# A decoder trunk on one core: fewer whole feed-forward tiles around the pairs, and the mixer's squares beside them

## The chip, the cores and the metric

The kernel runs on one core of a Trainium2 chip. The core has a matrix engine (TensorE, PE in the profile), three engines for elementwise work (VectorE or DVE, ScalarE or ACT, GpSimd or POOL), queues that issue transfers (the issues on SP and POOL matter here) and 16 DMA engines. The metric is the device time of one execution in microseconds (us), less is better. Each engine runs its instructions in the order in which the program was built, and an instruction that waits holds up all that stand behind it on its engine.

## The reference

A trunk of two layers on one sequence of 1024 tokens with 1024 channels, all in float32. Layer 0 mixes tokens with a causal convolution module, layer 1 with trailing means over windows of 2, 4, 8 and 16 tokens. Each mixer is followed by a SwiGLU feed-forward of width 2816. Each part is wrapped in an RMS norm, a shift and scale from a conditioning vector c, and a gated residual.

```python
for i in range(DEPTH):                       # 2 layers
    mod = silu(c) @ ada_w[i] + ada_b[i]
    sh_m, sc_m, g_m, sh_f, sc_f, g_f = split(mod, 6)
    h = rms_norm(x, norm_mix_g[i]) * (1 + sc_m) + sh_m
    y = conformer_conv(h, ...) if i == 0 else multiscale_pool(h, ...)
    x = x + (1 + g_m) * y
    h = rms_norm(x, norm_ffn_g[i]) * (1 + sc_f) + sh_f
    y = (silu(h @ w_gate) * (h @ w_up)) @ w_down        # 1024 -> 2816 -> 1024
    x = x + (1 + g_f) * y
return rms_norm(x, final_g)
```

## The kernel before, in words

**Halves.** The tokens are two chunks, A and B, of 512, held as x[chunk][k], eight tiles of 128 channels by 512 tokens. There are four feed-forward halves, and PE runs them in the order A0, B0, A1, B1 (chunk and layer). Between B0 and A1 lies A's pooling mixer, between A1 and B1 that of B. Work of the other chunk (its statistics, its mixer, a late piece of its feed-forward) is run inside a half.

**Products.** A float32 factor is split into a rounded part "hi" and a remainder "lo", and a product is three matmuls, hi·hi, hi·lo and lo·hi. The activations of a half are hhi and hlo (8 tiles each), those behind the SwiGLU ghi and glo. Each matmul is recorded at line 123, each operation of DVE, ACT and POOL at line 101, so the tiles' names (gate, up, dn, y, hhi, w, raw) tell the rows apart.

**Plain tiles.** The width is 22 f-tiles of 128. A plain f-tile (`ffn_p1`) is 24 matmuls of 512 columns for gate and 24 for up, then t = silu(gate) on ACT, t·up on DVE, ghi on ACT and glo on DVE or POOL. A down pass (`ffn_p2`) takes two f-tiles: eight output groups dn of 6 matmuls, each followed by an update of x on DVE. The weights of a plain tile come through `load_weight`: SP loads a tile raw (L398), ACT writes hi (a CAST) and minus raw (an ACTIVATE) into two of the nine buffers w, and POOL issues an accumulating load onto the second (L403), which leaves the lo part. ACT's write waits until PE has let go of the buffer.

**Pairs.** Between its first and its last plain tiles a half computes gate and up for two f-tiles at once by a 2×2 scheme with seven quarter products in place of eight ("f-pair" below; the gate or the up of one is a "mate", `ffn_pair`). A quarter product is 12 matmuls of 256 columns, so a mate is 84. It needs sums of quarters of the activations, called T (`combined`: hf = hi + lo, tf the sums, thi and tlo their parts, in rows k = 0 to 3; t1 to t4 are its columns), and sums of quarters of the weights (`Pair.prepare`: acc and ny on DVE from the raw tiles, then shi and slo; also two accumulating loads at L946). The first quarter product uses the activations as they are, the second already needs t1. Each mate carries four output groups of an earlier f-pair's down pass (24 matmuls of 512 columns). ACT copies the quarter products out of the accumulators (COPY t<-gate), DVE adds them.

**Order.** PE's order is that of the program text: a list of units (`unit`), each a tile, a down pass or a pair. `put` starts a task whose steps are spread beside the units that follow, when a planner's clocks for the engines let them (`pace`), and `need` asks that a task be done. The order on the other engines comes from a scheduler that ranks instructions by where they stand in the program. `PLAIN` is the count of whole tiles ahead of the pairs, `UNTIL` the tile at which a half's pairs end, `OUT_AT` the unit behind the pairs at which the mixer's output product y (`pool_out`) stands. `pool_stats` squares the other chunk's x on ACT, adds the squares on DVE into acc and starts the norm of its mixer: PE sums the columns (var), DVE takes the root (col), PE spreads it (rstd). `norm` does the same for a feed-forward and then makes hhi on ACT and hlo on DVE (`modulated`). Until B0's end DVE also computes layer 1's modulation (adaw, "ada dots" of 1024 columns, loaded at L133).

**Buffers.** `window` has three buffers shared by the mixer's sums, hf, sg and, in the change, pq; tag "acc" has two, shared by squares and by two of a mate's four weight sums.

Of the kernel before, what the change touches and what calls it, by code (L numbers as in the profile page):

```python
# [19 lines left out]
KT = D // P  # L20
# [26 lines left out]
STRETCH = 1.35  # L47
LATER = 300
PREPARED = 120
PLAIN = 4  # L50
UNTIL = (16, 16, 20)
OUT_AT = 6
DELAY = {"stats": 2.75, "spread": 1.5}
DELAY_BEHIND = {"stats": 8, "spread": 4}

# [51 lines left out]
def trunk(ctx, tc, xT, c, vec, ada, adan, w1, w2, wgu, wdn, wpl, out):  # L107
# [148 lines left out]
    def temp(n, name="t", bufs=0):  # L256
        t = tmp.tile([P, TMPW], F32, tag=name if bufs else "t", name=nm(name), bufs=bufs or 4)
        return t[:, :n]

    def window(n, name):  # L260

        t = tmp.tile([P, PHALO + TMPW], F32, tag="win", name=nm(name), bufs=3)
        return t[:, :n]
# [191 lines left out]
    class Squares:  # L455
# [5 lines left out]
        def add(self, k):  # L461
            ch = self.ch
            if self.acc is None:
                self.acc = bank("acc") if self.psum else temp(ch.n, "acc", 2)
                S_.activation(self.acc, x[ch.i][k], AF.Square)
            else:
                sq = temp(ch.n)
                S_.activation(sq, x[ch.i][k], AF.Square)
                was = self.acc
                if self.psum and k == KT - 1:  # L470
                    self.acc = temp(ch.n, "acc", 2)
                V_.tensor_tensor(self.acc, was, sq, op=ADD)

    def sum_sq(srcs, n):
        acc = None
        for s in srcs:
            if acc is None:
                acc = temp(n, "acc", 2)
                S_.activation(acc, s, AF.Square)
            else:  # L480
                sq = temp(n)
                S_.activation(sq, s, AF.Square)
                V_.tensor_tensor(acc, acc, sq, op=ADD)
            yield
        return acc
# [41 lines left out]
    def unit(emit, *weights):  # L527
        units.append((weights, emit))
# [333 lines left out]
    def combined(ch):  # L862

        other = chunks[1 - ch.i]
        h = st["h", ch.i]
        got = st["T", ch.i] = []
        for k in range(KT // 2):
            whole = []
            for hi, lo in (h[k], h[k + KT // 2]):
                t = window(ch.n, "hf")  # L870
                V_.tensor_tensor(t, f32(hi), f32(lo), op=ADD)
                whole.append(t)
            a, b = whole
            q12, q34 = temp(ch.n, "tf"), temp(ch.n, "tf")
            V_.tensor_tensor(q12[:, LEFT], a[:, LEFT], a[:, RIGHT], op=SUB)
            V_.scalar_tensor_tensor(q12[:, RIGHT], q12[:, LEFT], -1.0, b[:, RIGHT], op0=MUL, op1=SUB)
            V_.tensor_tensor(q34[:, LEFT], b[:, RIGHT], a[:, RIGHT], op=SUB)
            V_.scalar_tensor_tensor(q34[:, RIGHT], q12[:, RIGHT], -1.0, b[:, LEFT], op0=MUL, op1=SUB)
            yield
            row = []  # L880
            for q in (q12, q34):
                hi, lo = slot(other, "thi"), slot(other, "tlo")
                S_.copy(hi, q)
                V_.tensor_tensor(lo, q, f32(hi), op=SUB)
                row += [(hi[:, LEFT], lo[:, LEFT]), (hi[:, RIGHT], lo[:, RIGHT])]
            got.append(row)
            yield
# [184 lines left out]
    def ffn_mixed(ch, l, until, at_end=False):  # L1072

        before = []
        for f in range(0, PLAIN, 2):
            before += [ffn_p1(ch, l, f, True, False), ffn_p1(ch, l, f + 1, True, False)]
            if f:
                before.insert(-1, ffn_p2(ch, l, [f - 2, f - 1], True))
        mates = [Pair(ch, l, f, which) for f in range(PLAIN, until, 2) for which in range(2)]
        mine, theirs = [None] * len(mates), []  # L1080
        for i, f in enumerate(range(PLAIN - 2, until - 2, 2)):
            first, second = Downs(ch, l, (f, f + 1), (0, 1)), Downs(ch, l, (f, f + 1), (2, 3))
            for at, d in ((2 * i + 1, first), (2 * i + 2, second)):
                if at < len(mates):
                    mine[at] = d
                else:
                    theirs.append(d)
        last, = theirs
        paired = [(lambda take: mates[0].prepare(), ())]
        for i, me in enumerate(mates):  # L1090
            if i + 1 == len(mates):
                paired.append((lambda take: reserve.__setitem__(0, 2), ()))
            paired.append(ffn_pair(ch, l, me, mates[i + 1] if i + 1 < len(mates) else None, mine[i], (mine + [last])[i + 1]))
        paired.append((lambda take: last.load(last.dps[1]), ()))
        rest = ffn(ch, l, True, at_end, until, ffn_p2(ch, l, [until - 2, until - 1], True))
        rest[1:1] = [alone(last)]
        return before, paired, rest
# [123 lines left out]
    T = {}  # L1221

    def put(name, gen, urgent=False):
        def emit(take):
            T[name] = Task(gen(), urgent)
        unit(emit)

    def need(*names):
        unit(lambda take: finish(*(T[n] for n in names)))
# [58 lines left out]
    for i, (e, ws) in enumerate(fa):  # L1288
        if i == len(fa) - OUT_B:
            need("ln_b")  # L1290
            sq_b = Squares(B)
            conv_out(B, sq_b)
            unit(lambda take: T.__setitem__("norm_bf", Task(norm(B, 0, True, ("h", 1), squares=sq_b), True)))
        unit(e, *ws)
    need("norm_bf")
    unit(lambda take: stretch.__setitem__(0, 1.0))


    def pool_stats(ch):
        acc = yield from sum_sq(x[ch.i], ch.n)  # L1300
        steps = st["spread", ch.i] = mean_rsqrt(acc, ch.n, True, "col2")
        for said in steps:
            if said == "spread":
                break
            yield said
# [27 lines left out]
        need(("nf", ch.i))  # L1333
        unit(lambda take: st.__setitem__(("h", ch.i), st["hn", ch.i]))

    def paired(ch, us):
        need(("T", ch.i))
        add(us)

    before, pairs, rest = ffn_mixed(B, 0, UNTIL[0])  # L1340
    put(("T", 1), lambda: combined(B))
    add(before[:2])
    put(("stats", 0), lambda: pool_stats(A))
    add(before[2:])
    need(("stats", 0))
    paired(B, pairs)
    pooled(rest[:-1], A, OUT_AT)
    before, pairs, rest_a = ffn_mixed(A, 1, UNTIL[1])
    add(before[:1] + rest[-1:])
    put(("T", 0), lambda: combined(A))  # L1350
    add(before[1:2])
    put(("stats", 1), lambda: pool_stats(B))
    add(before[2:])
    need(("stats", 1))
    paired(A, pairs)
    pooled(rest_a[:-1], B, OUT_AT)
    before, pairs, rest = ffn_mixed(B, 1, UNTIL[2], True)
    add(before[:1] + rest_a[-1:])
    put(("T", 1), lambda: combined(B))
    add(before[1:])  # L1360
    put("final_a", lambda: final(A))
    paired(B, pairs)
    add(rest)
    run_units(W_BUFS, early)


# [42 lines left out]
```

## Time and profile before

| what | value |
|---|---|
| median of 3 runs | 1856.09 us (1854.83 to 1858.48) |
| the profiled execution | 1855.7 us, span 1853.9 us |
| mean granted TensorE clock | 0.983 |
| busy: PE, DVE, ACT, POOL | 95%, 72%, 56%, 32% of the span |
| norm of B0 (from its rstd at 714.0) and the late down passes of A0 | to 742.8 us |
| B0: whole tiles; pairs; whole tiles with A's mixer | 742.8 to 798.9; to 982.6; to 1102.1 us |
| A1: the same, with B's mixer | 1102.1 to 1169.3; to 1350.2; to 1468.7 us |
| B1: whole tiles; pairs; the rest | 1468.7 to 1535.5; to 1782.2; to 1853.9 us |

Times within the profile count from the first instruction. A row of the trace gives start, duration, engine, line, operation, output<-inputs, shape and, in brackets, how long the engine stood idle before it and what released it. PE's matmuls overlap in the records (each takes longer than the distance to the next), so its pace is read from starts.

### The profile page before, as it was taken

The page shows a single profiled execution, that of the slowest core. Times are in us where ns is not written, and L with a number is a line of the kernel's source. Part 1 is how long each engine was busy: PE and PEld are TensorE (multiplying, and loading weights), DVE is VectorE, ACT ScalarE, POOL GpSimd, SP SyncE. Part 2 cuts the span into 40 slices and gives each one's busy share as a digit, 9 for nine tenths or more (in the row PEclk, how much of TensorE's full clock was granted, in tenths as well). Part 3 has the DMA queues.
Part 4 walks back from the last instruction along what each step waited for, and adds up shares of the span by engine and source line. Part 5 has one row for each costly group of instructions (what it writes and reads, how often), then busy time and mean ns, then how long its engine had stood idle before and what let it go on. Part 6 is the DMA issues. An engine that isn't in the chain of part 4 may idle for free.

```text
span 1853.9 us, 25885 instructions
## 1 busy us (share of the span) xinstructions
PE 1770.2 (95%) x9544; PEld 1506.3 (81%) x9544; DVE 1325.7 (72%) x2147; ACT 1044.6 (56%) x1613; POOL 596.7 (32%) x636
## 2 busy tenths in 40 slices
PE   6999939999999999999999999999999999999996
PEld 4666628788888887889998788999988889999985
DVE  8788872897876326889978547778684468887736
ACT  3656645866665554655555555555555546555543
POOL 3478731777762311211115221111151221111111
PEclk9999959999999999999999999999999999999998
DMA  7968828889798798977765977655568876655562
GB/s 258 296 199 244 209 47 181 215 203 239 197 240 207 202 240 185 241 212 206 201 190 126 223 170 185 172 136 137 136 140 212 181 169 168 177 136 137 128 135 68
DMA packets 114801, 340.62 MB, mean 184 GB/s; under 512 B 11377, under 2 KB 21745, under 8 KB 114674
## 3 DMA queue, kind: packets, MB, share of 16 engines
q1 hardware_dynamic: 75792, 221.51, 35.9%
q0 software_dynamic: 37728, 116.41, 35.1%
q8 instruction: 75, 1.23, 0.3%
q10 hardware_dynamic: 1154, 1.05, 0.2%
q14 instruction: 52, 0.43, 0.1%
HBM read 334.73 MB, written 4.19 MB: 183 GB/s over the span
## 4 chain that ended last, share of the span: by engine, by line
PE 81%; DVE 7%; DMA 6%; issue 2%; ACT 2%; POOL 1%; SPq 0%; DVEq 0%; POOLq 0%; ACTq 0%
PE dn L123 22%; PE up L123 22%; PE gate L123 21%; PE y L123 6%; PE a L123 3%; PE g L123 2%; PE first L123 2%; DMA adaw<-in_adan_dram 2%; DMA raw<-in_wgu_dram 2%; DMA w<-in_wdn_dram 1%; DVE x L101 1%; ACT w L101 1%; DVE t L101 1%; DMA w<-in_wgu_dram 1%; PE ada L123 1%
## 5 line engine op out<-in xcount | busy, mean ns | idle before, releaser
L123 PE MATMUL dn<-ghi,w 128*128 128x512 f32 (+1 forms) x1440 | 471.4, 390 | 2.7 <-DMA w<-in_wdn_dram 1.3
L101 ACT ACTIVATE w<-raw 128x1024 fp32r<-128x1024 f32 (+1 forms) x262 | 243.0, 928 | 319.0 <-PE dn L123 95.9
L101 ACT CAST w<-raw 128x512 fp32r<-128x512 f32 (+1 forms) x392 | 322.3, 824 | 144.4 <-PE up L123 53.5
L101 DVE SCALAR_TENSOR_TENSOR x<-dn,gains,x 128x512 f32<-128x512 f32 (+1 forms) x360 | 263.1, 735 | 81.9 <-PE dn L123 79.1
L123 PEld LDWEIGHTS dn<-ghi,w 128*128 128x128 f32 x1440 | 270.7, 190 | 56.0 <-DMA w<-in_wdn_dram 2.1
L123 PE MATMUL gate<-hhi,w 128*128 128x512 f32 (+1 forms) x1088 | 310.8, 359 | 3.1 <-DMA w<-in_wgu_dram 2.6
L123 PE MATMUL up<-hhi,w 128*128 128x512 f32 (+1 forms) x1088 | 310.1, 358 | 0.0
L123 PE MATMUL dn<-glo,w 128*128 128x512 f32 (+1 forms) x720 | 279.9, 389 | 0.9 <-POOL glo L101 0.9
L101 POOL TENSOR_TENSOR pa<-pa,pr 128x512 f32<-128x512 f32 x175 | 239.0, 1445 | 24.4 <-ACT pr L101 21.9
L946 POOL DMA_DIRECT2D w<-in_wgu_dram x80 | 69.8, 872 | 493.4 <-ACT w L101 157.4
L123 PEld LDWEIGHTS gate<-hhi,w 128*128 128x128 f32 x1088 | 196.5, 189 | 35.4 <-DMA w<-in_wgu_dram 3.5
L123 PEld LDWEIGHTS up<-hhi,w 128*128 128x128 f32 x1088 | 196.7, 189 | 30.5
L123 PE MATMUL gate<-hlo,w 128*128 128x512 f32 (+1 forms) x544 | 195.1, 359 | 1.1 <-DVE hlo L101 1.1
L123 PE MATMUL up<-hlo,w 128*128 128x512 f32 (+1 forms) x544 | 194.6, 358 | 0.0
L403 POOL DMA_DIRECT2D w<-in_wgu_dram x96 | 86.5, 901 | 321.5 <-ACT w L101 297.8
L101 DVE SCALAR_TENSOR_TENSOR ca<-u,vecs,ca 128x512 f32<-128x512 f32 x273 | 186.6, 747 | 0.1
L101 DVE TENSOR_TENSOR t<-t,up 128x512 f32<-128x512 f32 (+1 forms) x88 | 55.0, 625 | 166.4 <-PE up L123 153.6
L123 PEld LDWEIGHTS dn<-glo,w 128*128 128x128 f32 x720 | 137.2, 191 | 23.8 <-POOL glo L101 1.2
L101 ACT ACTIVATE pr<-u,vecs 128x512 f32<-128x512 f32 x175 | 117.9, 716 | 13.4 <-POOL pa L101 5.9
L123 PEld LDWEIGHTS gate<-hlo,w 128*128 128x128 f32 x544 | 102.7, 189 | 17.6 <-DVE hlo L101 1.9
L123 PEld LDWEIGHTS up<-hlo,w 128*128 128x128 f32 x544 | 102.7, 189 | 15.6
L101 DVE TENSOR_TENSOR w<-raw,w 128x512 fp32r<-128x512 f32 (+1 forms) x122 | 84.5, 700 | 30.3 <-ACT w L101 27.2
(178 smaller groups left out, 3368.1 us busy)
## 6 DMA issues: line engine op xcount, KB each, us to landing
raw<-in_wgu_dram SPq DMA_DIRECT2D x176, 512.0 KB, 5.2
w<-in_wgu_dram POOLq DMA_DIRECT2D x96, 512.0 KB, 8.1
raw<-in_wdn_dram SPq DMA_DIRECT2D x88, 512.0 KB, 5.5
adaw<-in_ada_dram SPq DMA_DIRECT2D x64, 512.0 KB, 6.0
w<-in_wdn_dram POOLq DMA_DIRECT2D x48, 512.0 KB, 8.5
raw<-in_w_dram SPq DMA_DIRECT2D x44, 512.0 KB, 6.6
w<-in_wgu_dram POOLq DMA_DIRECT2D x80, 256.0 KB, 5.7
w<-in_w_dram POOLq DMA_DIRECT2D x34, 512.0 KB, 8.5
```

The source lines that it names most:

```text
L101: self.last = self.order(getattr(self.eng, name)(out, *args, **kw))
L123: last_mm[0] = nc.tensor.matmul(out, lhsT, rhs, start=start, stop=stop, **kw).ins.name
L403: order(nc.gpsimd.dma_start(as_src(lo), src, accum_op=ADD))
L946: order(nc.gpsimd.dma_start(lo, src, accum_op=ADD))
```

## The change

`PLAIN` goes from 4 to 2, `UNTIL` from (16, 16, 20) to (18, 18, 20), `OUT_AT` from 6 to 4. So each half has two whole tiles ahead of its pairs; B0 and A1 have four behind them, and B1 two as before. B0 and A1 have eight f-pairs in pair form in place of six each, and B1 nine in place of eight.

The three halves now go through one function, `segment`. In it the unit that is left over from the half before (`late`, the down pass of tiles 20 and 21) stands behind the first whole tile. For A1 and B1 that is its old place; for B0 it stood ahead of the norm's `need`, directly behind the other down passes of A0. T's task starts ahead of the first tile (it started behind the late pass in A1 and B1), T is asked for ahead of the pairs, and the squares of `pool_stats` start only then, beside the pairs, where they were beside the whole tiles. Their sum is a `window` called pq in place of a buffer acc.

What this does to DVE in B0, between the norm and the first pair. Before, behind the last updates of x by A0's tiles 18 and 19 (hf and tf make T; adaw is an ada dot):

```order
L101 SCALAR_TENSOR_TENSOR adaw_1060_5694,mod_136<-adaw_1060_5694,cact_75 128x1024
L101 SCALAR_TENSOR_TENSOR x_0_2_79<-dn_1134_6049,gains_137,x_0_2_79 128x512
L101 SCALAR_TENSOR_TENSOR x_0_3_80<-dn_1135_6057,gains_137,x_0_3_80 128x512
L101 TENSOR_TENSOR hf_1147_6114<-hhi_1079_5810,hlo_1080_5811 128x512
L101 TENSOR_TENSOR hf_1148_6116<-hhi_1087_5818,hlo_1088_5819 128x512
L101 SCALAR_TENSOR_TENSOR x_0_4_81<-dn_1136_6065,gains_137,x_0_4_81 128x512
L101 TENSOR_TENSOR tf_1149_6118<-hf_1147_6114 128x256
L101 TENSOR_TENSOR tf_1150_6119<-hf_1148_6116,hf_1147_6114 128x256
L101 SCALAR_TENSOR_TENSOR x_0_5_82<-dn_1137_6073,gains_137,x_0_5_82 128x512
L101 SCALAR_TENSOR_TENSOR tf_1149_6118<-tf_1149_6118,hf_1148_6116 128x256
```

In the changed kernel, from the same ada dot on:

```order
L101 SCALAR_TENSOR_TENSOR adaw_1060_5694,mod_136<-adaw_1060_5694,cact_75 128x1024
L101 TENSOR_TENSOR hf_1135_6062<-hhi_1079_5810,hlo_1080_5811 128x512
L101 TENSOR_TENSOR hf_1136_6064<-hhi_1087_5818,hlo_1088_5819 128x512
L101 TENSOR_TENSOR tf_1137_6066<-hf_1135_6062 128x256
L101 TENSOR_TENSOR tf_1138_6067<-hf_1136_6064,hf_1135_6062 128x256
L101 SCALAR_TENSOR_TENSOR tf_1137_6066<-tf_1137_6066,hf_1136_6064 128x256
L101 TENSOR_TENSOR acc_1203_6342<-raw_1172_6218 128x512
L101 TENSOR_TENSOR acc_1209_6354<-raw_1171_6216,raw_1172_6218 128x512
L101 SCALAR_TENSOR_TENSOR tf_1138_6067<-tf_1137_6066,hf_1136_6064 128x256
L101 SCALAR_TENSOR_TENSOR adaw_1097_5841,mod_136<-adaw_1097_5841,cact_75 128x1024
```

The updates by the late down pass have moved behind the start of T, and the weight sums of the first mate (acc from raw) and a second ada dot stand among T's first row.

ACT in A1, from the norm on. Before (ny is the spread rstd, hhi the eight activations, w the weights' parts):

```order
L101 COPY ny_1808_9613<-rstd_1807_9608 128x512
L101 ACTIVATE hhi_1768_9430<-t_1809_9615,mod_136 128x512
L101 ACTIVATE hhi_1770_9432<-t_1810_9619,mod_136 128x512
L101 ACTIVATE hhi_1772_9434<-t_1811_9623,mod_136 128x512
L101 ACTIVATE hhi_1774_9436<-t_1812_9627,mod_136 128x512
L101 ACTIVATE t_1815_9633<-gate_1800_9533 128x512
L101 ACTIVATE w_1833_9728<-raw_1831_9725 128x1024
L101 CAST w_1835_9734<-raw_1834_9732 128x1024
L101 ACTIVATE hhi_1776_9438<-t_1824_9666,mod_136 128x512
L101 CAST ghi_1813_9631<-t_1815_9633 128x512
L101 ACTIVATE hhi_1778_9440<-t_1825_9682,mod_136 128x512
L101 ACTIVATE hhi_1780_9442<-t_1826_9686,mod_136 128x512
```

In the changed kernel, from the first hhi on:

```order
L101 ACTIVATE hhi_1831_9781<-t_1872_9966,mod_136 128x512
L101 ACTIVATE hhi_1833_9783<-t_1873_9970,mod_136 128x512
L101 ACTIVATE hhi_1835_9785<-t_1874_9974,mod_136 128x512
L101 ACTIVATE hhi_1837_9787<-t_1875_9978,mod_136 128x512
L101 ACTIVATE t_1878_9984<-gate_1863_9884 128x512
L101 ACTIVATE w_1898_10082<-raw_1896_10079 128x1024
L101 CAST w_1901_10092<-raw_1900_10090 128x1024
L101 ACTIVATE w_1902_10093<-raw_1900_10090 128x1024
L101 CAST w_1929_10202<-raw_1928_10200 128x1024
L101 CAST ghi_1876_9982<-t_1878_9984 128x512
L101 ACTIVATE hhi_1839_9789<-t_1889_10035,mod_136 128x512
L101 ACTIVATE hhi_1841_9791<-t_1892_10055,mod_136 128x512
```

The fifth to eighth hhi stood behind two weight writes (the eighth a little later), and stand now behind four of them and a ghi. The order in B1 moves in the same way.

```diff
--- before.py
+++ after.py
@@ -47,9 +47,9 @@
 STRETCH = 1.35
 LATER = 300
 PREPARED = 120
-PLAIN = 4
-UNTIL = (16, 16, 20)
-OUT_AT = 6
+PLAIN = 2
+UNTIL = (18, 18, 20)
+OUT_AT = 4
 DELAY = {"stats": 2.75, "spread": 1.5}
 DELAY_BEHIND = {"stats": 8, "spread": 4}
 
@@ -1291,13 +1291,20 @@
             sq_b = Squares(B)
             conv_out(B, sq_b)
             unit(lambda take: T.__setitem__("norm_bf", Task(norm(B, 0, True, ("h", 1), squares=sq_b), True)))
-        unit(e, *ws)
+        if i < len(fa) - 1:
+            unit(e, *ws)
     need("norm_bf")
     unit(lambda take: stretch.__setitem__(0, 1.0))
 
 
     def pool_stats(ch):
-        acc = yield from sum_sq(x[ch.i], ch.n)
+        acc = window(ch.n, "pq")
+        S_.activation(acc, x[ch.i][0], AF.Square)
+        for k in range(1, KT):
+            yield
+            sq = temp(ch.n)
+            S_.activation(sq, x[ch.i][k], AF.Square)
+            V_.tensor_tensor(acc, acc, sq, op=ADD)
         steps = st["spread", ch.i] = mean_rsqrt(acc, ch.n, True, "col2")
         for said in steps:
             if said == "spread":
@@ -1333,34 +1340,27 @@
         need(("nf", ch.i))
         unit(lambda take: st.__setitem__(("h", ch.i), st["hn", ch.i]))
 
-    def paired(ch, us):
+    def segment(ch, l, until, late, at_end=False):
+
+        other = chunks[1 - ch.i]
+        before, pairs, rest = ffn_mixed(ch, l, until, at_end)
+        put(("T", ch.i), lambda: combined(ch))
+        add(before[:1] + late + before[1:])
         need(("T", ch.i))
-        add(us)
-
-    before, pairs, rest = ffn_mixed(B, 0, UNTIL[0])
-    put(("T", 1), lambda: combined(B))
-    add(before[:2])
-    put(("stats", 0), lambda: pool_stats(A))
-    add(before[2:])
-    need(("stats", 0))
-    paired(B, pairs)
-    pooled(rest[:-1], A, OUT_AT)
-    before, pairs, rest_a = ffn_mixed(A, 1, UNTIL[1])
-    add(before[:1] + rest[-1:])
-    put(("T", 0), lambda: combined(A))
-    add(before[1:2])
-    put(("stats", 1), lambda: pool_stats(B))
-    add(before[2:])
-    need(("stats", 1))
-    paired(A, pairs)
-    pooled(rest_a[:-1], B, OUT_AT)
-    before, pairs, rest = ffn_mixed(B, 1, UNTIL[2], True)
-    add(before[:1] + rest_a[-1:])
-    put(("T", 1), lambda: combined(B))
-    add(before[1:])
-    put("final_a", lambda: final(A))
-    paired(B, pairs)
-    add(rest)
+        if at_end:
+            put("final_a", lambda: final(other))
+        else:
+            put(("stats", other.i), lambda: pool_stats(other))
+        add(pairs)
+        if not at_end:
+            need(("stats", other.i))
+            pooled(rest[:-1], other, OUT_AT)
+            return rest[-1:]
+        add(rest)
+
+    late = segment(B, 0, UNTIL[0], fa[-1:])
+    late = segment(A, 1, UNTIL[1], late)
+    segment(B, 1, UNTIL[2], late, True)
     run_units(W_BUFS, early)
```

## The prediction

> **What bounds the kernel now.** I read the page's busy shares first, then the table of waits on TensorE (PE) for the part that the change touches, then the windows by stage, then single rows.
>
> ```profile
> PE 1770.2 (95%) x9544; PEld 1506.3 (81%) x9544; DVE 1325.7 (72%) x2147; ACT 1044.6 (56%) x1613; POOL 596.7 (32%) x636
> PE 81%; DVE 7%; DMA 6%; issue 2%; ACT 2%; POOL 1%; SPq 0%; DVEq 0%; POOLq 0%; ACTq 0%
> ```
>
> PE is busy 95% of the span, and the chain that ends last is PE for 81%. Next, what PE waits for from 717 us on (us in total, times, longest), and the windows (us; busy us and count on PE, PEld, DVE, ACT, POOL; clock; DMA share; GB/s):
>
> ```profile
> PE var L123 <- DVE acc L101: 6.4, 2, 4.6
> PE rstd L123 <- DVE col L101: 3.8, 2, 2.5
> PE gate L123 <- DMA w<-in_wgu_dram: 2.6, 2, 1.9
> PE gate L123 <- ACT t L101: 2.1, 1, 2.1
> ...
> 742.80:798.90 56.10, 55.77 (x249) 45.87 (x248) 46.13 (x86) 33.76 (x52) 16.58 (x18) 1.00 0.91 233
> 889.30:920.40 31.10, 31.10 (x217) 29.03 (x216) 28.50 (x48) 16.97 (x35) 4.83 (x7) 1.00 0.72 204
> 1200.00:1231.10 31.10, 31.10 (x219) 29.05 (x218) 24.73 (x41) 17.05 (x33) 3.48 (x4) 1.00 0.54 140
> ```
>
> These four, the largest, add up to 14.9 us of 1137, and the longest of them lie at the very end, which the change leaves alone. The granted clock is full (1.00). So two things can move the time: PE's own work, and new waits. The third row is one f-pair (two f-tiles of 128 columns) in pair form in half B0: PE is full, and DVE is busy 28.50 of 31.10 us, so DVE has little room there. In A1 (last row) it has 24.73.
>
> **Fewer matmul columns.** UNTIL less PLAIN gives (18−2)/2 + 8 + 9 = 25 f-pairs in pair form against 6+6+8 = 20. Spacings on PE:
>
> ```profile
> 736.17 0.39 PE L123 MATMUL dn<-glo,w 128*128 128x512 f32 x1
> 742.35 0.39 PE L123 MATMUL dn<-glo,w 128*128 128x512 f32 x1
> 804.23 0.28 PE L123 MATMUL gate<-tlo,shi 128*128 128x256 f32 x1
> 804.35 0.28 PE L123 MATMUL gate<-thi,slo 128*128 128x256 f32 x1
> 1102.14 0.39 PE L123 MATMUL gate<-hhi,w 128*128 128x512 f32 x1
> 1113.02 0.40 PE L123 MATMUL dn<-ghi,w 128*128 128x512 f32 x1
> ```
>
> Starts count, since the modelled ends overlap. A plain tile of gate and up is 48 matmuls, 1102.14 to 1113.02, 10.88 us; a down pass over two tiles is 48 matmuls at (742.35 − 736.17)/27 = 0.229, 10.99 us. A plain f-pair is thus 2 × 10.88 + 10.99 = 32.75. In pair form it is 168 matmuls of 256 columns (two mates of 7 × 12) and the same 48 downs, and the window at 889.30 shows 217 matmuls in 31.10, so 216 take about 31.06. The gain is 1.69 an f-pair, times five **−8.45**.
>
> The Trainium skill, "TensorE: Matmul & The Clock Gate", section "Back-to-back issue gap", gives a sustained 81 ns a matmul at 128 columns and 131 ns at 512 for a stream with weight loads; an estimate between them of some 97 ns at 256 would make pair form dearer (168 × 97 against 96 × 131 ns, 3.7 us an f-pair), and five f-pairs +18.6 in place of −8.45. The trace differs, 227 ns at 512 and 120 ns at 256 columns, and its spacings decide.
>
> **B0, from the norm to the first pair.** The late down pass of tiles 20 and 21 of A0 (2 weight loads on SP, 4 casts on ACT, 2 accumulating loads on POOL, 48 matmuls, 8 updates on DVE) moves behind the first tile of B0, and two plain tiles and a down pass go. PE stands thus before:
>
> ```profile
> 729.86 0.40 PE L123 MATMUL dn<-ghi,w 128*128 128x512 f32 x1
> 731.24 0.51 PE L123 MATMUL dn<-ghi,w 128*128 128x512 f32 x1 [0.99 <-ACT ghi L101]
> 732.62 0.49 PE L123 MATMUL dn<-glo,w 128*128 128x512 f32 x1 [0.87 <-POOL glo L101]
> 804.01 0.38 PE L123 MATMUL gate<-thi,shi 128*128 128x256 f32 x1 [2.06 <-ACT t L101]
> ```
>
> The moved pass loses its two waits (1.38 − 0.23 = 1.15 each, −2.3), since its operands are then ten us old. PE starts B0's gate at 729.3, the late pass at 740.2, the second tile at 751.2, the first pair at 762.0; 12 matmuls of its first quarter product and 9 of the second later, at 764.5, it wants the last row of t1 from DVE. DVE's order before that row has 64 instructions after the update that ends at 731.65: 6 ada dots, 8 updates, 16 of 256 columns and 34 of 512. Their spacings:
>
> ```profile
> 730.25 1.40 DVE L101 SCALAR_TENSOR_TENSOR x<-dn,gains,x 128x512 f32<-128x512 f32 x2
> 735.43 1.22 DVE L101 SCALAR_TENSOR_TENSOR adaw<-adaw,cact 128x1024 f32<-128x1024 f32 x1
> 736.57 0.08 DVE L101 DVE_READ_ACCUMULATOR adaw<-adaw,cact 128x1 f32 x1
> 740.04 0.42 DVE L101 TENSOR_TENSOR tf<-hf 128x256 f32<-128x256 f32 x1
> 740.38 0.42 DVE L101 TENSOR_TENSOR tf<-hf,hf 128x256 f32<-128x256 f32 x1
> 771.83 0.68 DVE L101 TENSOR_TENSOR acc<-acc,t 128x512 f32<-128x512 f32 x1
> 772.43 0.68 DVE L101 TENSOR_TENSOR ny<-acc,raw 128x512 f32<-128x512 f32 x1
> 732.18 0.33 SPq L398 DMA_DIRECT2D raw<-in_wgu_dram  x1
> raw<-in_wgu_dram SPq DMA_DIRECT2D x176, 512.0 KB, 5.2
> 786.51 0.69 DVE L101 TENSOR_TENSOR acc<-raw 128x512 f32<-128x512 f32 x1 [4.36 <-DMA raw<-in_wgu_dram]
> ```
>
> The dot is 736.57 − 735.43 = 1.14, the update 1.40 − 0.74 = 0.66, the narrow one 0.34, the wide one 0.60: 6 × 1.14 + 8 × 0.66 + 16 × 0.34 + 34 × 0.60 = 38.0, so 769.6. Among them stand the sums of the first mate's weights, reached at 735.0, and their raw tile is issued only at about 732.2 and lands 5.2 later: 2.4 more, and behind that waiting instruction stands all of T. That makes 772.1, a wait of 7.6 for PE. Without the DMA part it is 5.2; with the 4.36 that such a sum waited at 786.51, 9.6. I take 7.6, since the median landing is of just this kind of load. The old start of the pairs had 2.1 at 804.01 (for a copy on ACT), and this vanishes under the longer wait. Net 7.6 − 2.3 − 2.1 = **+3.2** (0.8 to 5.2).
>
> **A1, from the norm to the first pair.** Between rstd and the gate of A1 there stood two plain tiles (the first begun) and a down pass:
>
> ```profile
> 1079.35 0.83 PE L123 MATMUL rstd<-ident,col 128*128 128x128 f32 x6
> 1082.62 2.71 ACT L101 ACTIVATE hhi<-t,mod 128x512 fp32r<-128x512 f32 x4 [0.82 <-DVE t L101]
> 1101.43 1.06 ACT L101 ACTIVATE w<-raw 128x1024 fp32r<-128x1024 f32 x1 [6.00 <-PE dn L123]
> 1104.29 1.03 ACT L101 CAST w<-raw 128x1024 fp32r<-128x1024 f32 x1
> 1114.76 0.73 PE L123 MATMUL dn<-ghi,w 128*128 128x512 f32 x2 [0.42 <-DMA w<-in_wdn_dram]
> 1481.79 0.73 PE L123 MATMUL dn<-ghi,w 128*128 128x512 f32 x2 [0.85 <-DMA w<-in_wdn_dram]
> ```
>
> Before, all eight hhi stood ahead of the block of weight casts that waits for the last down group (1101.43, four casts, done at 1105.3, 3.2 after the gate's start at 1102.14). With one tile less behind rstd, ACT's order has that block, and a ghi, between hhi 4 and hhi 5. At some 0.6 each for the ghi and the hhi (four took 2.71 at 1082.62), hhi 5 is done 4.4 after the gate's start and its hlo, after a hand-over to DVE, at 5.6, while PE wants that hlo after 13 matmuls, at 2.95: 2.65. Of the next three, whose hlo on DVE stand among sums of raw weights, the sixth adds 0.65, the seventh 1.5 (behind such a sum) and the eighth 0.55: **5.4** in all; with no sum in the way 3.9, with a raw tile 3 us late 8.4. The late pass behind that tile loses its 0.4 (1114.76). The squares, now beside the pairs, put two adds ahead of what ACT's first copies of the quarter products wait for: +1.5 (0 to 3). Net 5.4 − 0.4 + 1.5 = **+6.5** (3.5 to 11.0).
>
> The Trainium skill speaks against this step: the same page, section "Architectural detail: the array is 16× 32×32, not 1× 128×128", has ACT and DVE as strict first-in first-out queues, so that no hhi passes a waiting cast. The trace agrees: ACT stood idle for the 6.00 us ahead of 1101.43, whatever stood behind that cast. Were it otherwise, the sum would be that of rival (a).
>
> **B1, from the norm to the first pair.** The same order on ACT; without the two sums among the hlo it is 3.9 and 0.4 for the later eighth, 4.3, and the 0.9 at 1481.79 goes: **+3.4** (1 to 5). T is far enough ahead here and in A1, as DVE has no ada dots left.
>
> **The mixers and the pairs.** OUT_AT of 4 puts y some 39 us behind the pairs' end instead of 63:
>
> ```profile
> 982.56 1.05 PE L123 MATMUL rstd<-ident,col 128*128 128x128 f32 x8
> 1024.26 0.73 PE L123 MATMUL gate<-hhi,w 128*128 128x512 f32 x2 [1.88 <-DMA w<-in_wgu_dram]
> 1025.92 0.69 DVE L101 TENSOR_TENSOR mxlo<-win,mxhi 128x512 fp32r<-128x512 f32 x1 [0.17 <-ACT mxhi L101]
> 1045.81 0.39 PE L123 MATMUL y<-mxhi,w 128*128 128x512 f32 x1
> ```
>
> The last mxlo is done 44 us behind 982.56, and y's last group wants it some 48 behind: nothing on the path, with 4 us to spare; the 2.0 at 1024.26 passes to another weight. The squares (7 adds at 0.60 on DVE, 8 on ACT, and a dozen tiny ones) and five more f-pairs' 28 DVE instructions each lie beside pairs with 2.6 us (B0) or 6.4 (A1) of room an f-pair; I put +0.5 on B0 (0 to 3), where the room is least.
>
> **Sum.** −8.45 + 3.2 + 6.5 + 3.4 + 0.5 = +5.15. The profiled execution took 1855.7 (span 1853.9 and 1.8 around it), 0.4 below the median of 1856.1; on the profiled execution that makes 1860.9, from the median 1861.2.
>
> **Rivals.** (a) Faster: ACT's blocks of casts find their buffers free early, so that hhi 5 to 8 are never held. For it: ACT was idle for 6.00 us ahead of 1101.43, so it has the time. Against it: the block stands on the last down group directly ahead of the gate. It gives 5.15 − 5.4 − 4.3 = −4.55, 1851.5; it decides once the block ends 2.65 us earlier. (b) No change: the raw tile is early at B0 (5.2 in place of 7.6), the first mate of A1 has its 1.5 hidden and A1's sum is not in the way: 5.15 − 2.4 − 1.5 − 1.5 = −0.25, 1855.8. For it: the plain stages are the busiest for DMA (share 0.91 at 742.80), and the change loads less there; against it: the raw tile waits for ACT, not for DMA. (c) Worse: DVE runs full through B0's pairs. 28.50 of 31.10 leaves 2.6 an f-pair, and a sum that waits for its raw tile, as the 4.36 at 786.51, uses it up: if three f-pairs miss by 2, +6, 1867.2. (d) The 256-column matmuls space at 0.1295, where 168 of them cost the 21.76 of the plain form and the −8.45 is gone: 5.15 + 8.45 = +13.6, 1869.7. The rows have 0.12, so hardly. The Trainium skill's "Back-to-back issue gap" ("TensorE: Matmul & The Clock Gate") speaks for this one.
>
> **How the numbers follow.** Forecast 0.57, (a) 0.14, (b) 0.15, (c) 0.12, (d) 0.02. A measurement here tells 0.2%, 3.7 us, from no change. The forecast's own range is 1857 to 1865, a fifth of it below 1859.8. So slower 0.46 + 0.12 + 0.02 = 0.60; same 0.11 + 0.14 = 0.25; faster 0.15. The range of 1852 to 1867.5 leaves out half of (a) and of (c), and (d).
>
> **What would show it.** PE's rows of 256 columns 840 more and those of 512 columns 480 fewer; gaps of 5 to 10 us in B0's second quarter product, released by DVE tlo, and of 4 to 6 in the gates of A1 and B1, released by DVE hlo; no wait at the late down passes; DVE over 29 of 31 us in B0's pairs if (c). I am wrong if the gates of A1 and B1 run through, or if y waits for mxlo.

## The result and the profile after

The changed kernel takes 1866.22 us (median of 8 runs, 1862.82 to 1875.58); the kernel before, over 8 runs, 1854.66 (1852.59 to 1858.48). The ratio is 1.0071, with a 95% interval of 1.0051 to 1.0090: slower by 13 us, between 9.5 and 16.7. The forecast was slower by 5.15.

The page of the changed kernel (busy time and share of each engine) and PE's waits from 700 us on (us in total, times, longest):

```profile
PE 1768.5 (95%) x9904; PEld 1519.5 (81%) x9904; DVE 1405.3 (75%) x2286; ACT 1060.2 (57%) x1698; POOL 584.1 (31%) x622
...
PE var L123 <- DVE acc L101: 6.6, 2, 4.8
PE gate L123 <- DVE hlo L101: 5.7, 5, 3.5
PE y L123 <- DMA w<-in_wpl_dram: 4.3, 2, 3.5
PE rstd L123 <- DVE col L101: 3.8, 2, 2.5
PE gate L123 <- ACT t L101: 3.7, 1, 3.7
PE gate L123 <- DVE tlo L101: 3.3, 2, 2.6
PE gate L123 <- ACT hhi L101: 2.9, 2, 1.4
PE gate L123 <- ACT thi L101: 2.6, 2, 1.9
```

The rows for var and rstd stood there before; the six others are new or have grown. PE's work fell as forecast: one f-pair of B0 is again 31.1 us, now with the squares beside it, and DVE is no fuller (28.70 here, 28.50 before):

```profile
820.00:851.06 31.06, 31.06 (x219) 29.00 (x218) 28.70 (x55) 17.06 (x34) 2.73 (x4) 1.00 0.67 186
```

Where the time came from, stage by stage, from the starts of PE's rows. "More" is the stage's length after less that before, with the plain f-pair (32.75 us) that left it, and var (0.81) where it moved, added back. Both kernels were profiled a second time (e11 and e12 below), so there are two pairs of traces:

| stage | forecast | first traces | second traces |
|---|---|---|---|
| ahead of B0's norm (rstd) | 0 | −6.3 | −0.3 |
| fewer columns, five f-pairs | −8.45 | −8.45 (counted) | −8.45 (counted) |
| B0, rstd to the end of the first mate | +3.2 | +6.2 | +5.7 |
| A1, gate to the end of the first mate | +6.5 | +13.4 | +11.0 |
| B1, gate to the end of the first mate | +3.4 | +5.3 | +3.2 |
| the stretches behind the pairs, with y | 0 | +2.0 | +4.3 |
| the rest | +0.5 | −1.2 | −0.6 |
| span, after less before | +5.15 | +10.9 | +14.9 |

For example B0: 757.63 + 20.31 − 707.72 = 70.22 after, 798.93 + 12.74 − 714.04 = 97.63 before; −27.41 + 33.56 = +6.2. The first row looks like chance: PE does the same up to there, and B0's norm began at 714.0 and 710.8 in two traces of the kernel before, at 707.7 and 710.5 in two of the changed one, and between 707.2 and 712.2 in the ten variants below.

A1 is the largest. ACT, then PE, then DVE of the changed kernel:

```profile
1099.83 1.06 ACT L101 ACTIVATE w<-raw 128x1024 fp32r<-128x1024 f32 x1 [3.42 <-PE dn L123]
...
1102.69 1.03 ACT L101 CAST w<-raw 128x1024 fp32r<-128x1024 f32 x1
1103.62 0.61 ACT L101 CAST ghi<-t 128x512 fp32r<-128x512 f32 x1
1104.14 1.95 ACT L101 ACTIVATE hhi<-t,mod 128x512 fp32r<-128x512 f32 x3
...
1100.56 0.39 PE L123 MATMUL gate<-hhi,w 128*128 128x512 f32 x1
...
1104.91 0.50 PE L123 MATMUL gate<-hhi,w 128*128 128x512 f32 x1 [1.45 <-ACT hhi L101]
1106.22 0.50 PE L123 MATMUL gate<-hlo,w 128*128 128x512 f32 x1 [0.80 <-DVE hlo L101]
...
1111.99 0.79 PE L123 MATMUL gate<-hlo,w 128*128 128x512 f32 x1 [3.48 <-DVE hlo L101]
...
1110.58 0.69 DVE L101 TENSOR_TENSOR acc<-raw 128x512 f32<-128x512 f32 x1 [2.15 <-DMA raw<-in_wgu_dram]
1111.19 0.75 DVE L101 SCALAR_TENSOR_TENSOR hlo<-t,mod,hhi 128x512 fp32r<-128x512 f32 x1
```

The block of weight writes starts 0.73 us ahead of the gate, the ghi follows, and hhi 5 comes 3.6 us into the gate: the mechanism that was forecast, at its place. The seventh hlo stands on DVE behind a weight sum that waits for its raw tile, and that is the longest wait of the gate.

### The profile page after: what moved, and what is told of

The parts are those of the page before. It is cut to its first block, busy times and chain, and to the rows that moved or that the text cites. A ratio compares the mean times of both kernels' runs of the same rounds, so it can differ in the third digit from the quotient of the medians.

```text
span 1864.8 us, 26834 instructions
## 1 busy us (share of the span) xinstructions
PE 1768.5 (95%) x9904; PEld 1519.5 (81%) x9904; DVE 1405.3 (75%) x2286; ACT 1060.2 (57%) x1698; POOL 584.1 (31%) x622
## 4 chain that ended last, share of the span: by engine, by line
PE 83%; DVE 8%; DMA 4%; ACT 2%; issue 1%; POOL 1%; SPq 0%; DVEq 0%; POOLq 0%; ACTq 0%
PE dn L123 23%; PE gate L123 23%; PE up L123 22%; PE y L123 6%; PE a L123 3%; PE first L123 2%; DMA adaw<-in_adan_dram 2%; PE g L123 2%; DVE x L101 1%; DVE t L101 1%; DMA w<-in_wpl_dram 1%; ACT w L101 1%; DVE hlo L101 1%; PE ada L123 1%; DVE acc L101 1%
## 5 line engine op out<-in xcount | busy, mean ns | idle before, releaser
L101 ACT ACTIVATE w<-raw 128x1024 fp32r<-128x1024 f32 (+1 forms) x252 | 223.8, 888 | 245.1 <-PE up L123 66.4
L123 PE MATMUL gate<-hhi,w 128*128 128x512 f32 (+1 forms) x1008 | 279.4, 351 | 2.9 <-ACT hhi L101 2.9
L123 PE MATMUL up<-hhi,w 128*128 128x512 f32 (+1 forms) x1008 | 276.3, 348 | 0.0
L123 PEld LDWEIGHTS gate<-hhi,w 128*128 128x128 f32 x1008 | 182.5, 192 | 28.6 <-ACT hhi L101 3.7
L123 PEld LDWEIGHTS up<-hhi,w 128*128 128x128 f32 x1008 | 180.7, 190 | 25.0
L123 PE MATMUL gate<-hlo,w 128*128 128x512 f32 (+1 forms) x504 | 178.0, 353 | 6.8 <-DVE hlo L101 6.8
L123 PE MATMUL up<-hlo,w 128*128 128x512 f32 (+1 forms) x504 | 175.5, 348 | 0.0
L101 DVE TENSOR_TENSOR t<-t,up 128x256 f32<-128x256 f32 (+1 forms) x88 | 53.7, 610 | 121.4 <-PE up L123 111.8
L101 DVE TENSOR_TENSOR w<-raw,w 128x512 fp32r<-128x512 f32 (+1 forms) x152 | 104.7, 695 | 33.9 <-ACT w L101 30.0
L101 ACT CAST shi<-ny 128x512 fp32r<-128x512 f32 x100 | 62.0, 620 | 119.3 <-PE gate L123 60.4
```

The source lines that it names most:

```text
L101: self.last = self.order(getattr(self.eng, name)(out, *args, **kw))
L123: last_mm[0] = nc.tensor.matmul(out, lhsT, rhs, start=start, stop=stop, **kw).ins.name
```

## The experiments

**e1: the two feed-forward norms urgent.** Only the order of the norms' steps changes, on ACT (hhi) and on DVE (t and hlo) alike.

```diff
-                put(("nf", ch.i), lambda: norm(ch, 1, True, ("hn", ch.i), True))
+                put(("nf", ch.i), lambda: norm(ch, 1, True, ("hn", ch.i), True), True)
```

> The changed kernel with one word more: the task of the two feed-forward norms (A1 and B1) is urgent, so its steps are issued as soon as rstd is there and ACT has all eight hhi ahead of the block of weight casts that waits for the last down group. Theory one (hhi 5 to 8 behind that block make the waits in the gates): the first gate of A1 falls from 13.73 us to 5.5 to 7, that of B1 from 10.86 to about 5.5, the rows at half clock right behind them go, and the time falls by 10 to 14 us against the changed kernel, to 1852 to 1856. Rival (the hlo wait in any case, because DVE is held by the raw weight tile and by T): the gates keep 3 us or more of waits each and the time stays above 1860.

Measured: 1855.87 us, ratio to the kernel before 0.9991 (0.9980 to 1.0003), where the change alone has 1.0071. The gate of A1, first matmul of gate and first of up:

```profile
1106.57 0.39 PE L123 MATMUL gate<-hhi,w 128*128 128x512 f32 x1
...
1112.01 0.39 PE L123 MATMUL up<-hhi,w 128*128 128x512 f32 x1
```

5.44 us, no wait, and the same in B1 (1471.63 to 1477.07). So the order of the norm's steps makes both gates wait, and moving them alone carries the change from slower to even. The rival's waits did not come, but its cause was not tested, since e1 moved the hlo too: on DVE all eight now stand ahead of the raw weight's sums, as on ACT the hhi stand ahead of the block of weight writes:

```profile
1093.01 2.05 ACT L101 ACTIVATE hhi<-t,mod 128x512 fp32r<-128x512 f32 x3 [0.27 <-DVE t L101]
...
1094.22 2.73 DVE L101 SCALAR_TENSOR_TENSOR hlo<-t,mod,hhi 128x512 fp32r<-128x512 f32 x4
```

So e1 does not tell ACT's block from DVE's sum. The rows of the changed kernel above do: 1.45 and 0.80 us behind the late hhi, 3.48 us behind the sum on DVE. The first mate of A1 fell as well, from 15.51 to 10.89; e9 below has 10.92 with the gates late, so this fall is not shown to be the norm's doing.

**e2: the new order with the old numbers.**

```diff
-PLAIN = 2
-UNTIL = (18, 18, 20)
-OUT_AT = 4
+PLAIN = 4
+UNTIL = (16, 16, 20)
+OUT_AT = 6
```

> The changed kernel's order of units and its squares beside the pairs, but with the numbers of before (PLAIN 4, UNTIL 16, 16, 20, OUT_AT 6), so the same matmuls as before. Theory one (the waits come from having two whole tiles fewer around the starts): the gates of A1 and B1 run through at 5.44, B0 loses the two waits of its late down pass, and the time is that of before within 3 us. Rival (the order itself costs, by T ahead of the first tile and the squares among the pairs): 5 us or more above before, with waits at the first pair of A1 as in the changed kernel (3.9 us).

Measured: 1861.50 us, 1.0030 (1.0017 to 1.0043). The gates of A1 and B1 run through, as theory one said, but the order does cost some 5 us, and not where the rival put it: A1's first mate is 10.01, B0's is 20.68, as long as in the changed kernel, although it stands behind two more tiles. PE, ACT and the queue of SP there:

```profile
803.29 0.58 PE L123 MATMUL gate<-thi,shi 128*128 128x256 f32 x1 [7.78 <-ACT t L101]
...
797.74 0.62 ACT L101 CAST w<-raw 128x512 fp32r<-128x512 f32 x1 [9.02 <-DMA raw<-in_wdn_dram]
...
777.53 13.09 SPq L133 DMA_DIRECT2D adaw<-in_ada_dram  x2
790.72 0.47 SPq L967 DMA_DIRECT2D raw<-in_wdn_dram  x1
```

Two loads for ada dots hold SP for 13 us; DVE's next dot, which frees a buffer, ends at 790.3, just before the down weights are issued. These land late; ACT waits for them, and the squares and the first copy of a quarter product stand behind that.

**e3: the new numbers in the old order.** The kernel before with the three numbers of the change.

```diff
-PLAIN = 4
-UNTIL = (16, 16, 20)
-OUT_AT = 6
+PLAIN = 2
+UNTIL = (18, 18, 20)
+OUT_AT = 4
```

> The kernel before with the three new numbers alone (PLAIN 2, UNTIL 18, 18, 20, OUT_AT 4); the late pass of B0 ahead of its norm, T behind the late pass, and the squares before the pairs, asked for ahead of them. Theory one: the gates of A1 and B1 wait as in the changed kernel (some 8 and 5 us), since the tile that is missing behind rstd is the cause, and the starts of the pairs wait for T and for the squares, 8 us or more each in B0 and A1: 1866 to 1880. Rival (the order is what costs): 1850 or less, by the 8.45 us of fewer columns.

Measured: 1892.89 us, 1.0194 (1.0175 to 1.0212). The gates of A1 and B1 wait (8.95 and 13.93 us long), so the missing tiles cause that in either order. The larger part is that two tiles do not hide the squares where they stood: PE waits for their sum, ahead of the pairs, 10.4 us in B0 and 16.6 in A1. The squares beside the pairs go with the smaller `PLAIN`.

**e4: matmuls that nothing reads, in the waits.** Rows of half clock (a spacing of 0.43 us at 512 columns in place of 0.227) stand behind the waits of the changed kernel; e4 keeps PE at work.

```diff
+                        if l == 1 and f == 0 and o is outs[0] and k == 4:
+                            fill("fill", wt[0], h[0][0], 36 if ch.i == 0 else 24, ch.n)
                         products(o, wt, k, h[k], k == 0, k == KT - 1)
...
+            n_fill = {(1, 0): 60, (0, 1): 32}.get((ch.i, l), 0) if me.f == PLAIN and me.which == 0 else 0
+            if n_fill:
+                fill("fill", w11[0], b11[0][0], n_fill, H)
             quad(right, s1, t1, True)
```

> The changed kernel with matmuls added that nothing reads, at three of the places where PE waits longest: 36 of 512 columns (8.2 us) ahead of the fifth step of A1's first gate, 24 (5.4 us) at that of B1, 60 of 256 columns (7.2 us) ahead of the second quarter product of B0 and 32 (3.8 us) at that of A1. PE then stays at work while DVE and ACT catch up. Theory of the clock (after a wait of some us PE runs at half clock for 3 to 6 us, and that adds to the wait): the rows at half clock go, and the time falls by 4 to 9 us against the changed kernel although PE has 24.6 us more work. Rival (the waits alone set it, the half clock falls into time in which PE would wait anyway): the same time within 2 us, or longer.

Measured: 1866.34 us, 1.0065 (1.0038 to 1.0093), as the changed kernel. The clock (the third column from the end) behind the wait of A1 in the changed kernel, and over the whole first gate of A1, filler included, in e4:

```profile
1112.00:1114.00 2.00, 2.00 (x5) 1.47 (x6) 2.00 (x5) 0.00 (x0) 0.00 (x0) 0.50 0.02 4
```

```profile
1103.90:1118.20 14.30, 14.06 (x62) 11.25 (x62) 11.26 (x19) 6.96 (x10) 3.04 (x3) 1.00 0.64 147
```

The half clock is gone and no time is gained. For A1 that says little: the filler takes 8.2 us where the waits were 7.1 by the starts, so gate and up take 19.63 us with the filler in them, 19.61 without. B1's fell from 17.44 to 16.35. B0 says more: its filler takes 7.2 us, T's last row is 7.4 us late without it, and behind the filler PE waits for copies on ACT where the changed kernel has rows at half clock:

```profile
775.34 0.39 PE L123 MATMUL gate<-thi,shi 128*128 128x256 f32 x1 [1.35 <-ACT t L101]
779.19 0.39 PE L123 MATMUL gate<-thi,shi 128*128 128x256 f32 x1 [0.73 <-ACT t L101]
```

Its first mate takes 20.12 us with the filler, 20.31 without. So PE at half clock seems there mostly to pass time in which the next operand is missing.

**e5: the ada dots held in B0.** On top of e1.

```diff
+        if l == 0:
+            unit(lambda take: setattr(T["ada", 1], "until", 1e9))
         put(("T", ch.i), lambda: combined(ch))
         add(before[:1] + late + before[1:])
         need(("T", ch.i))
+        if l == 0:
+            unit(lambda take: setattr(T["ada", 1], "until", 0.0))
```

> The kernel of e1 (changed kernel, urgent feed-forward norms), and between B0's norm and its first pair the task of the ada dots is held, so that neither its six dots on DVE nor its loads on SP stand there; it goes on beside the pairs. Theory one (B0's wait is DVE's list ahead of T, of which the dots are 6 x 1.14 = 6.8 us, and the loads that queue on SP behind them): the waits at the late pass and in the first mate of B0, 4.4 and 9.5 us in e1, fall by 6 to 9 us together, and the time by as much, to 1847 to 1850. Rival (the raw weight tile of the first mate holds DVE in any case, or the dots that come later press on the pairs): less than 3 us of gain, or new waits among the pairs of B0.

Measured: 1845.69 us, 0.9941 (0.9926 to 0.9956): the fastest kernel of the study, 11 us ahead of the one before. B0's first mate falls from 19.50 to 12.81 us; what is left of its wait is ACT's, not T's:

```profile
768.93 0.39 PE L123 MATMUL gate<-thi,shi 128*128 128x256 f32 x1 [2.54 <-ACT t L101]
```

The late pass is 15.64 as in e1 (15.40), so holding the dots does not shorten it, and the gain is in the mate. The dots fit beside the pairs.

**e6: the late pass back ahead of B0's norm,** on top of e1.

```diff
-        if i < len(fa) - 1:
-            unit(e, *ws)
+        unit(e, *ws)
...
-    late = segment(B, 0, UNTIL[0], fa[-1:])
+    late = segment(B, 0, UNTIL[0], [])
```

> The kernel of e1 with the late down pass of A0 back ahead of B0's norm being asked for, as in the kernel before. Theory one (the move is worth the two waits of 1.15 us and nothing else, since T has the same DVE list ahead of it either way): the late pass has its two waits again, the start of the pairs waits as before or up to 3 us less, and the time is within 3 us of e1. Rival (the move put the late pass's eight updates and two weight loads into T's way and is what makes the first mate of B0 wait): the first mate's waits fall by 5 us or more and the time with them.

Measured: 1858.36 us, 1.0012 (1.0001 to 1.0022), by the ratios 4 us above e1. The two waits of 1.15 are back, and the first mate is 20.66, no shorter. The rival falls; the move of the late pass is worth some 4 us (each ratio is known to some 2 us), a little more than its two waits.

**e7: the squares beside the whole tiles,** on top of e1.

```diff
-        add(before[:1] + late + before[1:])
+        add(before[:1])
+        if not at_end:
+            put(("stats", other.i), lambda: pool_stats(other))
+        add(late + before[1:])
         need(("T", ch.i))
         if at_end:
             put("final_a", lambda: final(other))
-        else:
-            put(("stats", other.i), lambda: pool_stats(other))
```

> The kernel of e1 with the squares started behind the first whole tile again, where the kernel before has them, and all else as in e1. Theory one (the squares beside the pairs cost ACT and DVE the start of the first mate): the first mate of A1 and of B0 lose 0.5 to 2 us of their waits, and the time falls by 1 to 3 us. Rival (two whole tiles are too few to carry the squares and T, so the squares beside the pairs are the better place): new waits ahead of the first pair, 3 us or more above e1.

Measured: 1853.05 us, 0.9988 (0.9977 to 0.9998), by its interval not to be told from e1. The first mates are 19.17 and 11.86, against 19.50 and 10.89. Neither theory holds: as long as nothing asks for the squares ahead of the pairs, their start does not matter here.

**e8: e2 with the ada dots held,** by the four lines that e5 adds.

> The kernel of e2 (new order, numbers of before), with the ada dots held between B0's norm and its first pair as in e5. In e2 PE waited 7.9 us in the first mate of B0 for a copy on ACT, behind a cast that waited for a down weight whose load stood on SP behind two ada loads. Theory one (the ada task blocks SP, and with it the pair's weights): the first mate of B0 runs within 2 us of 10.0, and the time falls by 6 to 9 us against e2, to or below the kernel before. Rival (the squares on ACT are what the copy stands behind): the wait stays above 5 us.

Measured: 1852.17 us, 0.9986 (0.9969 to 1.0004). B0's first mate takes 10.01 us, with no wait. So the ada task costs the new order its 5 us. The rows of e2 point to SP and those of the changed kernel to DVE's list; holding the task takes both away and does not part them. Between e8 and e5 lie the five f-pairs and the urgent norms that these need: 0.9986 − 0.9941 is 8.3 us, which fits the 8.45 of fewer columns (each of the two ratios is known to some 3 us).

**e9: the changed kernel with the dots held,** the four lines of e5 without the line of e1.

> The changed kernel with the ada dots held between B0's norm and its first pair, and the norms of A1 and B1 as the change has them. If the two causes are independent, B0's first mate runs near 13 us in place of 20.3, the gates of A1 and B1 still wait some 8 and 5 us, and the time is that of the changed kernel less 6 to 9 us, 1857 to 1860. If they share a cause (DVE being late from B0 on), the gates of A1 and B1 shorten too and the time is below 1853.

Measured: 1857.28 us, 1.0009 (0.9999 to 1.0019). B0's first mate is 15.11 and the gates stay at 13.97 and 10.86, so the dots do not make the gates wait: the two causes are independent there. The first mate of A1 is 10.92. By the ratios the two steps bring some 12 us (held) and 15 us (urgent), and 24 together in e5.

**e10: e4 with less filler,** one execution (1861.43 us).

```diff
-                            fill("fill", wt[0], h[0][0], 36 if ch.i == 0 else 24, ch.n)
+                            fill("fill", wt[0], h[0][0], 24 if ch.i == 0 else 12, ch.n)
...
-            n_fill = {(1, 0): 60, (0, 1): 32}.get((ch.i, l), 0) if me.f == PLAIN and me.which == 0 else 0
+            n_fill = {(0, 1): 24}.get((ch.i, l), 0) if me.f == PLAIN and me.which == 0 else 0
```

> The filler of e4 cut below the waits: 24 matmuls of 512 columns (5.4 us) in A1's first gate, 12 (2.7 us) in that of B1, 24 of 256 (2.9 us) in the first mate of A1, none in B0. Theory of the clock (what PE loses at half clock is added to the waits): gate and up of A1 together take 18.7 us or less in place of 19.61, those of B1 16.0 or less in place of 17.44, the first mate of A1 14.2 or less in place of 15.51, and no row stands at half clock there. Rival (PE at half clock only passes time in which the next hlo or copy is not there yet): the three take what they take in the changed kernel within 0.5 us.

Measured: gate and up 21.40 in A1 and 15.28 in B1, the first mate 13.23. In A1 the seventh hlo came so late that PE waited 3.0 us behind the filler and fell to half clock again; in B1 no row is at half clock and 2.2 us are won. But e11, with no filler, has 15.57 in B1 and 12.85 in the mate, so neither fall proves anything. What the half clock costs at one place stays open between nothing and some 2 us; it is not shown to be a cause of the 13, and not shown to be none.

**e11 and e12: both kernels again,** one execution each (1868.78 and 1853.63 us).

> The changed kernel once more, for a second trace of it. Waits that the instruction order sets (hhi 5 to 8 behind the weight casts in A1 and B1, T behind DVE's list in B0) should be the same to a few tenths: gate of A1 from 12 to 14 us, of B1 10.9, the first mate of B0 19.5 to 20.5. Waits that a transfer sets should differ: the 3.9 us in the first mate of A1, the 3.6 in y, the seventh hlo of A1. If the 3.9 is the squares' doing it stays, if it is a late load's or a chance of the clock it changes by more than 1 us.

> The kernel before once more, for a second trace. The stages from B0's norm on should repeat within 1 us each, while the start of that norm, 714.0 us in the first trace, differs by up to 7 us between kernels whose programs are alike up to there (707.2 to 714.0 so far); if it stays at 714 here, that part belongs to the change and not to chance.

Measured: gate of A1 14.21 (13.73), of B1 10.11 (10.86), first mate of B0 19.41 (20.31). These belong to the order, to about 1 us. The first mate of A1 is 12.85 (15.51), and its wait changed from 3.7 to 2.6 us by the rows, so by the sign that was set the squares alone do not make it. The kernel before repeats to within 1 us behind B0; B0 itself, from rstd to the end of the first mate, took 97.6 and 100.2 us, which the expectation did not have. The longest wait in y of the changed kernel is again some 3 us, and the wait for the seventh hlo of A1 is 3.30:

```profile
1118.51 0.52 PE L123 MATMUL gate<-hlo,w 128*128 128x512 f32 x1 [3.30 <-DVE hlo L101]
1154.47 0.39 PE L123 MATMUL gate<-thi,shi 128*128 128x256 f32 x1 [2.58 <-ACT t L101]
```

## Why the prediction was wrong in size

**Fewer columns, −8.45: right.** The f-pairs take the 31.06 us counted, and e8 against e5 gives 8.3.

**A1, +6.5: right cause, wrong size, and the main error.** Gate and up wait 8.7 and 9.5 us in the two traces (19.61 and 20.39 against 10.88) where 5.4 stood in the sum. By the starts the fifth hlo came 2.7 us late in both (2.65 in the working), and the sixth added 0.6 and 0.8 (0.65). The step needs ACT to keep its order; the prediction calls that a point against it, but it is one for it, and the rows bear it out. The term that failed is the seventh hlo, put at 1.5: it added 3.8 and 4.1 us (3.48 and 3.30 of them idle), because the weight sum ahead of it on DVE waited 2.15 and 2.66 us for a raw tile. The step's own upper bound of 8.4, for a raw tile 3 us late, was near the case that happened. Rows of half clock behind that wait, which the working did not have, end the gate and up later still, by some 1.6 us in the first trace; e4 and e10 could not part the two.

The first mate of A1 then took 5.5 and 2.8 us more than 10.01, where 1.5 stood in the sum. PE waited 3.7 and 2.6 us there for a copy, which stands on ACT behind casts and the squares (t<-x). In the changed kernel:

```profile
1144.77 1.15 ACT L101 ACTIVATE t<-x 128x512 f32<-128x512 f32 x2
...
1147.89 0.63 ACT L101 ACTIVATE t<-x 128x512 f32<-128x512 f32 x1
1148.42 0.62 ACT L101 COPY t<-gate 128x256 f32<-128x256 f32 x2
```

What sets its size stays open: e1 has 10.89 with the gate on time, but e9 has 10.92 with the gate as late as here.

**B0, +3.2: half of what came.** T was right: its last tlo reached PE 7.4 us late in both traces (767.64 and 773.37, against 22 spacings of 0.12 from the mate's start), 7.6 in the working. In the changed kernel:

```profile
761.80 0.38 PE L123 MATMUL gate<-thi,shi 128*128 128x256 f32 x1 [1.87 <-ACT thi L101]
764.83 0.58 PE L123 MATMUL gate<-tlo,shi 128*128 128x256 f32 x1 [2.65 <-DVE tlo L101]
...
766.40 0.58 PE L123 MATMUL gate<-thi,shi 128*128 128x256 f32 x1 [0.77 <-ACT thi L101]
767.64 0.58 PE L123 MATMUL gate<-tlo,shi 128*128 128x256 f32 x1 [0.66 <-DVE tlo L101]
```

What failed are the two waits that were subtracted. The first mate took 20.3 and 19.4 us, 10.3 and 9.4 above 10.01: behind T another 2.9 and 2.0 us went by with rows at half clock, and in e4, without them, in waits for copies on ACT. So the 2.1 us wait for such a copy seems not to have vanished under T's. And the late pass did not lose its waits. It waits 1.7 to 4.7 us, for other reasons than before: its output buffers come free by DVE's updates, and these now stand among T. In e11, DVE and PE:

```profile
745.52 1.22 DVE L101 SCALAR_TENSOR_TENSOR adaw<-adaw,cact 128x1024 f32<-128x1024 f32 x1
...
746.66 0.74 DVE L101 SCALAR_TENSOR_TENSOR x<-dn,gains,x 128x512 f32<-128x512 f32 x1
...
747.47 0.50 PE L123 MATMUL dn<-ghi,w 128*128 128x512 f32 x1 [2.00 <-DVE x L101]
```

The working moved the pass with all its instructions past T, and counted its eight updates as T's delay, but not T as the delay of the updates and so of PE.

**B1, +3.4: right** in the second traces (3.2), 1.9 too low in the first (5.3), where PE stood at half clock for longer. **The stretches behind the pairs, 0: too low by 2 to 4.** The 2.0 us wait for a weight did pass to y's weight, but is 3.5 there, and 3.0 in the second trace:

```profile
1055.35 0.73 PE L123 MATMUL y<-mxhi,w 128*128 128x512 f32 x2 [3.46 <-DMA w<-in_wpl_dram]
```

y did not wait for mxlo. **The squares:** where they start costs little (e7), but in A1 they stand ahead of the copy that PE waited for. **Rival (c), DVE full through the pairs, fell:** 28.70 of 31.06 us. **Rival (a)** was right that ACT has the time: e1 gives it by the order alone.

A mistake in method may stand behind part of this. The raw tile in A1 and the weight in y were each taken at a likely landing, and both came later in both traces; two traces do not show how often. That the range, 1852 to 1867.5, holds the measured time is in part luck: its upper end makes room for half of rival (c), which did not happen, while A1's two traces lie at and above the bound of 11.0 that its step gave, and B0's lie above its 5.2.

## What to carry to other kernels

When whole tiles are taken from between a norm and its first use, look in each elementwise engine's order at what stands between the norm's steps and that use: on the in-order ACT a write that waited 3.42 us for a buffer, and on DVE a sum that waited 2.15 us for its tile, became a wait for everything behind it. Ask as well which background task shares a queue with the weights of the next stage; here holding its loads on SP and its dots on DVE brought some 12 us (e9), more than the 8.45 that fewer columns were to bring. With the norms urgent and the ada task held (e5), the same change is 0.6% ahead of the kernel before in place of 0.7% behind it. The kernel before was not run with these two steps; e8, the nearest to that, is at 0.9986.

## What was not expected of the hardware

Behind waits of PE that came close together the granted clock stood at 0.50 for some microseconds, and matmuls of 512 columns came at 0.43 us in place of 0.227 (1112 to 1115 us in A1, the window quoted under e4). The Trainium skill, "TensorE: Matmul & The Clock Gate", section "HAM oscillation — how this bites in real kernels", tells of such a fall to half clock behind idle gaps over about 3.4 us; the trace agrees for the gap of 3.48 at 1111.99. Elsewhere no run here shows such a limit: the wait of 3.46 us at 1055.35, in y, was followed by no slow row in that trace, while that of 3.01 at the same place in e11 was, and in B0's first mate the clock stood at 0.50 from 763.7 to 773.7 us although no single wait there was longer than 2.65. Taking the slow rows away with unread matmuls about as long as the waits (e4) did not shorten the kernel.
